# One layer of a hybrid attention and state-space network: decay rows read from HBM and merged by a masked copy, a rotary turn by halves, a later division, silu(z) kept in HBM

## The chip, the cores and the metric

The kernel runs on one core of a Trainium2 chip. The metric is the device time of one execution in microseconds; the figure given is the median of three runs. The core has a matmul engine (TensorE, PE in the profile, with its weight loads as PEld), a vector engine (VectorE, DVE), an activation engine (ScalarE, ACT), a general engine (GpSimd, POOL), a queue that mostly issues DMAs (SyncE, SP) and 16 DMA engines. SBUF is its working memory, PSUM the memory that matmuls write, HBM the large memory outside.

## The reference

One layer on 512 latent tokens of width 1024, with a prefix of 256 context tokens; all in float32, depth 1. Cut to what matters:

```
h = modulate(rms_norm(x), shift, scale) @ w_in      # cq, ckv, kr, z, xbc, dt; the same for the context
# 16 attention heads: 64 columns without and 32 with rotary position, 512 queries on 768 keys
q_rope = q_rope * cos + rotate_half_axial(q_rope) * sin
p = softmax((q_nope @ k_nope.T + q_rope @ k_rope.T) * SCALE);  attn = p @ v
# 16 state-space heads, forward and backward, chunks of 128 tokens
cum = cumsum(dt * A)                                # within a chunk
y = (C B^T * tril(exp(cum_t - cum_s))) @ (dt * xs)  # y_diag: decay inside a chunk, per head and direction
  + exp(cum_t) * (C @ entering_state)               # y_off
y = y_forward + flip(y_backward) + d * xs
ssd = rms_norm(y * silu(z))
x = x + gate * rms_norm(concat(attn, ssd) @ w_out)
x = x + gate * rms_norm((gelu(conv(g)) * v) @ w_down)   # gated MLP, g and v from one product with w_up
```

The forward decay of a head is nonzero for s <= t, the backward one for s >= t; both hold the diagonal s = t.

## The kernel before, in words

Almost every product is made in three passes of float32r matmuls: a helper `split` (L495 to L498) cuts an operand into a high part (ScalarE copies it) and a low part (VectorE subtracts), and high x high, high x low and low x high are added up in PSUM. So each operand costs ScalarE and VectorE one pass over it. Transposes and a few small products run on unsplit float32.

The program is written as generators. It is traced twice: the first trace collects all instructions, then `plan` (L381) schedules them by its own price list, orders each engine's instructions and gives every tile a place in SBUF. Memory is counted in units of 256 float32 columns; `t2` takes two units and `t4` four, UNITS is their number. The written order decides which tile may follow which in a place; the order of the instructions on each engine is the plan's.

The stages in order: modulation and the z part of the input projection (`silu_of_z`, L687, keeps the values of silu(z), doubled, in four `t4` tiles `z` until the scan ends); the other parts of the projection; then two generators beside each other (`beside`, L453): `group_sums`, the scan of both groups of eight state-space heads with `ssd_finish`, and `projections`, the rest of the input projection and then eight pairs of attention heads. `beside(main, other, pace)` steps the second by the weight that the first yields, times `pace`. After both comes the output projection (`natural_gemm`, attention's rows first), the gated MLP's up products and its down products.

The places that the change touches:

- The decay of head h on two chunks (L1019 to L1040). Two matmuls with `sel` spread the rows of the running sums `chl` (a high and a low part) over 128 partitions, for the two directions (L1025). A third one (L1029, identity x `caps`) adds -1e30 where a direction has no decay. ScalarE takes the exponential of four 128x128 blocks with a bias by column (L1034), GpSimd adds the two directions (L1038), VectorE multiplies with C B^T (L1039). The result `M` is the operand of y_diag (L1058).
- The states (L997 to L1018) are computed first; the entering states of all chunks and directions are kept, and their products (L1048 to L1054) are made after the decays, beside y_diag. `y` is `z` itself, multiplied in place (L1062).
- The rotary turn of the queries (L1119 to L1126): a float32 matmul with a matrix `rot` of zeros, ones and minus ones per two head pairs (L1122), then products with cosine and sine and their sum.
- The attention of a head (L1167 to L1182): scores in PSUM, their largest value (VectorE, L1177), the exponential and its sum (ScalarE, L1179), the reciprocal (L1181) and the division of the 128x768 weights by it (GpSimd, L1182), then six transposes (L1193), a split, and the product with V (L1205).
- The rows of the modulation (`modfinish`, L1267): a column tile of 8 values on 128 partitions goes to HBM in single words and comes back as a row on all partitions, both issued by GpSimd.

## Time and profile before

| what | value |
|---|---|
| three runs | 999.69, 1001.02, 1004.33 us |
| median | 1001.02 us |
| span of the profiled execution (first to last instruction) | 994.4 us |
| mean granted clock of TensorE | 0.990 |
| DVE, ACT, POOL busy | 700.9, 501.4, 259.5 us |
| DMA | 116.88 MB, 118 GB/s in the mean |

The page gives the span of the profiled execution and no device time of its own, so the span stands beside the runs. In the groups of instructions a row reads: line, engine, operation, tile written<-tiles read, their shapes, count | busy us, mean ns of one | idle us of the engine before them, and what ended it. An engine's busy time counts overlapping instructions once; matmuls follow each other more closely than their duration says. A line such as L498 is a helper's and stands for all its callers; the shapes tell these apart.

### The profile page before, as it was taken

The numbers are of one execution on the slowest core, as the hardware profiler recorded it, in microseconds if no ns is written. First come the engines' busy times: TensorE is split into PE (matmuls) and PEld (weight loads), VectorE is DVE, ScalarE is ACT, GpSimd is POOL, SyncE is SP. The second block draws the span as 40 slices with busy tenths as digits, with TensorE's granted clock in tenths as the row PEclk, the third lists the DMA queues.
The fourth block names the chain that finished last, engine by engine and source line by source line (L and its number), as shares of the span: only waits on it lengthen the run. The fifth ranks groups of instructions, "written<-read, shape, count | busy, mean of one in ns | idle before, by whom it ended". The sixth has DMA issues, their size and how long they took to land.

```text
span 994.4 us, 14412 instructions
## 1 busy us (share of the span) xinstructions
PE 971.8 (98%) x5224; PEld 825.9 (83%) x5224; DVE 700.9 (70%) x1304; ACT 501.4 (50%) x994; POOL 259.5 (26%) x223
## 2 busy tenths in 40 slices
PE   9999999999998999999999999999999999999996
PEld 8888888888876888888888888888888888888885
DVE  5999866988896989978789997952515442773406
ACT  4545337568566787687787324842314323452101
POOL 0001001765697886656541000000000000000000
PEclk7999999999998999999999999999999999999999
DMA  9922101012222242331566965431223221354422
GB/s 350 362 74 85 53 1 44 22 48 81 67 57 54 56 111 78 99 74 46 153 259 230 323 160 199 148 127 64 106 85 106 106 85 43 110 177 137 158 76 84
DMA packets 42214, 116.88 MB, mean 118 GB/s; under 512 B 5776, under 2 KB 8736, under 8 KB 42144
## 3 DMA queue, kind: packets, MB, share of 16 engines
q1 hardware_dynamic: 41440, 114.30, 34.8%
q0 software_dynamic: 528, 1.59, 0.5%
q8 instruction: 41, 0.67, 0.3%
q14 instruction: 29, 0.24, 0.1%
q10 hardware_dynamic: 176, 0.09, 0.0%
HBM read 96.02 MB, written 4.21 MB: 101 GB/s over the span
## 4 chain that ended last, share of the span: by engine, by line
PE 49%; DVE 6%; DMA 4%; issue 2%; ACT 1%; SPq 0%; POOL 0%; DVEq 0%; ACTq 0%; POOLq 0%
PE banks L751 26%; PE banks L1476 12%; PE banks L1175 4%; PE banks L1205 3%; PE banks L1193 2%; DVE block L498 2%; DMA block<-block 1%; DMA mod_rows<-mod 1%; DVE block L586 1%; PE banks L1109 1%; DMA block<-mod_rows 1%; ACT block L1179 1%; DVE smalls L1177 1%; DMA block<-in_wmod_dram 0%; DVE smalls L524 0%
## 5 line engine op out<-in xcount | busy, mean ns | idle before, releaser
L751 PE MATMUL banks<-block,block 128*128 128x512 f32 (+1 forms) x2132 | 448.3, 360 | 1.7 <-DVE block L1385 1.1
L751 PEld LDWEIGHTS banks<-block,block 128*128 128x128 f32 x2132 | 358.8, 188 | 62.5 <-issue 1.6
L498 DVE TENSOR_TENSOR block<-block,block 128x512 fp32r<-128x512 f32 (+5 forms) x252 | 227.0, 923 | 125.7 <-PE banks L751 47.8
L497 ACT ACTIVATE block<-block 128x512 fp32r<-128x512 f32 (+5 forms) x252 | 181.4, 743 | 207.8 <-PE banks L751 48.1
L1476 PE MATMUL banks<-block,block 128*128 128x512 f32 x496 | 116.6, 389 | 0.0
L1182 POOL TENSOR_TENSOR block<-block,smalls 128x768 f32<-128x768 f32 x64 | 97.3, 1527 | 60.7 <-DVE smalls L1181 38.4
L1476 PEld LDWEIGHTS banks<-block,block 128*128 128x128 f32 x496 | 93.0, 188 | 19.5
L1175 PE MATMUL banks<-block,block 128*128 128x512 f32 (+1 forms) x384 | 95.1, 357 | 1.4 <-DMA block<-block 0.7
L1276 POOL DMA_DIRECT2D mod_rows<-mod x3 | 2.9, 975 | 351.4 <-DVE mod L1272 351.4
L498 DVE TENSOR_TENSOR block<-banks,block 128x256 fp32r<-128x256 f32 (+1 forms) x156 | 83.2, 555 | 14.7 <-ACT block L497 12.9
L497 ACT ACTIVATE block<-banks 128x256 fp32r<-128x256 f32 (+1 forms) x156 | 73.0, 498 | 32.4 <-PE banks L1193 17.7
L1289 PE MATMUL banks<-block,block 128*128 128x512 f32 x384 | 88.6, 390 | 0.0
L1289 PEld LDWEIGHTS banks<-block,block 128*128 128x128 f32 x384 | 71.8, 188 | 14.5
L1193 PE MATMUL banks<-cst,block 128*128 128x128 f32 x384 | 66.9, 279 | 4.1 <-DVE block L498 3.7
L1205 PE MATMUL banks<-block,block 128*128 128x256 f32 x384 | 68.7, 299 | 0.8 <-DVE block L498 0.8
L1175 PEld LDWEIGHTS banks<-block,block 128*128 128x128 f32 x384 | 59.6, 190 | 10.2 <-ACT block L1179 2.7
L586 DVE SCALAR_TENSOR_TENSOR block<-block,block 128x1024 f32<-128x1024 f32 x52 | 62.6, 1219 | 4.1 <-DMA block<-in_wmod_dram 1.9
L1177 DVE TENSOR_REDUCE smalls<-banks 128x1 f32<-128x768 f32 x64 | 60.8, 950 | 6.6 <-PE banks L1175 5.9
L1179 ACT ACTIVATE block<-banks,smalls 128x768 f32<-128x768 f32 x64 | 57.7, 902 | 13.2 <-DVE smalls L1177 7.6
L786 DVE SCALAR_TENSOR_TENSOR block<-banks,cwh,block 128x510 f32<-128x510 f32 (+3 forms) x88 | 51.1, 620 | 14.4 <-ACT block L782 13.9
L1205 PEld LDWEIGHTS banks<-block,block 128*128 128x128 f32 x384 | 55.9, 191 | 5.3 <-DVE block L498 1.1
L1193 PEld LDWEIGHTS banks<-cst,block 128*128 128x128 f32 x384 | 47.7, 143 | 14.1 <-DVE block L498 3.9
(216 smaller groups left out, 1064.1 us busy)
## 6 DMA issues: line engine op xcount, KB each, us to landing
block<-in_wmod_dram SPq DMA_DIRECT2D x48, 512.0 KB, 6.9
block<-in_wup_dram SPq DMA_DIRECT2D x44, 512.0 KB, 3.8
block<-in_wdn_dram SPq DMA_DIRECT2D x44, 256.0 KB, 2.8
block<-block SPq DMA_DIRECT2D x32, 256.0 KB, 3.0
block<-in_wout_dram SPq DMA_DIRECT2D x16, 512.0 KB, 5.9
block<-block SPq DMA_DIRECT2D x56, 128.0 KB, 2.3
block<-in_wxbc_dram SPq DMA_DIRECT2D x12, 512.0 KB, 3.4
block<-in_wz_dram SPq DMA_DIRECT2D x16, 256.0 KB, 7.1
```

The costliest lines, as they stand in the source:

```text
L497: act(hi, src, AF.Copy)
L498: (lo_eng or V).tensor_tensor(out=lo, in0=src, in1=hi, op=ALU.subtract)
L586: V.scalar_tensor_tensor(out=junk, in0=wt, scalar=0.5, in1=vec, op0=ALU.mult, op1=ALU.mult, accum_out=acc)
L751: mm(po, lhsT=wf(k, pt[0]), rhs=xf(k, pt[1]), start=(k == 0 and pt == parts[0]), stop=(k == nk - 1 and pt == parts[-1]))
L1175: mm(sc[:, o : o + n], lhsT=q_[:, x_, qi * P : (qi + 1) * P], rhs=kk[:, y_, :], start=part == 0, stop=part == 2)
L1177: V.reduce_max(nm, sc[:, :T], axis=AX.X, negate=True)
L1179: act(pe, sc[:, :T], AF.Exp, bias=nm, scale=1.0, accum_out=sm_)
L1182: G.tensor_tensor(out=pe, in0=pe, in1=sm_.to_broadcast([P, T]), op=ALU.mult)
L1193: nc.tensor.transpose((tx if c < NX else tc_)[:, o : o + P], pe[:, s_ : s_ + P], ident)
L1205: mm(po[:, half * 256 : half * 256 + 256], lhsT=vst(c), rhs=rhs, start=(part == 0 and c == 0), stop=(part == 1 and c == NKT - 1))
L1289: mm(po[i][:, nh * 512 : nh * 512 + 512], lhsT=l[lp][:, i * P : (i + 1) * P], rhs=w[wp][:, nh * 512 : nh * 512 + 512], start=(k == 0 and l ...
L1476: mm(po[i], lhsT=l[lp][:, i * P : (i + 1) * P], rhs=w[wp], start=(k == 0 and lp == 0 and wp == 0), stop=(k == NF - 1 and lp == 1))
```

## The change

Five edits and what belongs to them:

- Decays. The running sums of both directions are copied to HBM as 32 rows (`cum_rows`). For each head and pair of chunks a DMA brings the head's two rows, spread over all partitions, as a tile of 128 x 2 x 256. VectorE adds to the forward part, for each chunk, a column (`nbd`, the difference of the two directions' biases), then a masked copy puts the forward part over the backward one where s <= t. ScalarE takes the exponential of the two merged blocks with the backward bias, GpSimd multiplies with C B^T. The backward term of the diagonal, which the merged decay no longer holds, goes into the factor of xs: dt_backward x diag(C B^T) + d (`skip`).
- The products with the entering states are made as soon as a state is known, and added up in `yc`; the states are not kept.
- Rotary. The 32 rotary columns of queries and keys are reordered in the weights so that the partner of a row lies 64 partitions away; two VectorE products of half height read one half of PSUM and write the other. Each head's rotary rows are then copied in two pieces.
- Division. The exponentials go undivided into the product with V. The eight sums of a pair of heads are inverted at once, stored to HBM in single words, read back as rows and multiplied into the 128x512 result by GpSimd.
- silu(z) is stored to HBM when it is made and read back, 128x512 at a time, where `y` is formed.

The rows of the modulation are issued by ScalarE's queue. UNITS goes from 200 to 212 and the scratch of dynamic DMAs to 4096 bytes; the pace of `beside` goes from 1.0 to 1.5. The mask matrices `capf` and `capb` go. The diff, cut to its core:

```diff
-UNITS, EDGE, MARGIN = 200, 168, 2500
+UNITS, EDGE, MARGIN = 212, 168, 2500
+PACE, MW = 1.5, 1.5
...
-        zi = z[i][:, nh * 512 : nh * 512 + 512]
+        zi = t2()
         act(zi, po[i], AF.Tanh, scale=0.5)
         V.scalar_tensor_tensor(out=zi, in0=zi, scalar=1.0, in1=po[i], op0=ALU.add, op1=ALU.mult)
+        load(gate[nh, i], zi)
...
-    act(chl[:32], pq[:32], AF.Copy)
-    V.tensor_tensor(out=chl[32:64], in0=pq[:32], in1=chl[:32], op=ALU.subtract)
+    act(cumT, pq[:32], AF.Copy)
+    load(cumR.rearrange("d h t -> (d h) t"), cumT)
...
                 if n >= 2:
-                    entering[dir_][c] = state[dir_]
+                    ep = t2(P, 512, dt=F32R), t2(P, 512, dt=F32R)
+                    split(*ep, state[dir_], V)
+                    pO = pget("s")
+                    for part, (i, j_) in enumerate(((0, 0), (1, 0), (0, 1))):
+                        mm(pO, lhsT=cp_[:, i, c * P : (c + 1) * P], rhs=ep[j_], start=part == 0, stop=part == 2)
...
-                pdf = pget("s")
-                for dir_ in range(2):
-                    mm(pdf[:, dir_ * 256 : dir_ * 256 + 256],
-                       lhsT=sel[:, dir_ * 16 + h : dir_ * 16 + h + 1].to_broadcast([P, P]),
-                       rhs=chl[:, cp2 * 256 : cp2 * 256 + 256], start=dir_ == 0, stop=False)
-                mm(pdf, lhsT=capi, rhs=caps, start=False, stop=True)
-                df = t2()
-                for dir_ in range(2):
-                    for j in range(2):
-                        o = (dir_ * 2 + j) * P
-                        act(df[:, o : o + P], pdf[:, o : o + P], AF.Exp,
-                            bias=nb[:, cp2 * 2 + j, dir_ * 16 + h : dir_ * 16 + h + 1])
-                G.tensor_tensor(out=Me, in0=df[:, :256], in1=df[:, 256:], op=ALU.add)
-                V.tensor_tensor(out=Me, in0=Me, in1=cbt[:, cp2 * 256 : cp2 * 256 + 256], op=ALU.mult)
+                df, at = t2(P, 2, 256), slice(cp2 * 256, cp2 * 256 + 256)
+                load(df, cumR[:, h, at].unsqueeze(0).to_broadcast([P, 2, 256]))
+                for j in range(2):
+                    V.tensor_scalar(out=cols(0, j), in0=cols(0, j), scalar1=nbd[:, cp2 * 2 + j, h : h + 1], scalar2=None, op0=ALU.add)
+                V.copy_predicated(df[:, 1, :].rearrange("p (c n) -> p c n", c=2), later, df[:, 0, :].rearrange("p (c n) -> p c n", c=2))
+                for j in range(2):
+                    act(cols(1, j), cols(1, j), AF.Exp, bias=nb[:, cp2 * 2 + j, 16 + h : 17 + h])
+                G.tensor_tensor(out=M[e // 4][:, e % 4, :], in0=df[:, 1, :], in1=cbt[:, at], op=ALU.mult)
...
-                G.tensor_tensor(out=y[c][:, gs], in0=y[c][:, gs], in1=ya, op=ALU.mult)
+                zl = t2()
+                load(zl, gate[g, c])
+                G.tensor_tensor(out=y[c][:, gs], in0=zl, in1=ya, op=ALU.mult)
...
+            for to, of in ((slice(0, 64), slice(64, 128)), (slice(64, 128), slice(0, 64))):
+                V.tensor_tensor(out=qsn[to], in0=pq[of], in1=C("sin")[to], op=ALU.mult)
             pfree(pq)
-            pr = pget("p")
-            mm(pr, lhsT=C("rot"), rhs=qr, start=True, stop=True)
-            V.tensor_tensor(out=qsn, in0=pr, in1=C("sin"), op=ALU.mult)
...
-            r0 = ((hp % 2) * 2 + j) * 32
-            nc.sync.dma_start(out=r32(qt[j][64:96]), in_=r32(qrs[r0 : r0 + 32]))
+            r0 = ((hp % 2) * 2 + j) * 16
+            for o in range(2):
+                nc.sync.dma_start(out=r32(qt[j][64 + 16 * o : 80 + 16 * o]), in_=r32(qrs[64 * o + r0 : 64 * o + r0 + 16]))
...
-        act(pe, sc[:, :T], AF.Exp, bias=nm, scale=1.0, accum_out=sm_)
+        act(pe, sc[:, :T], AF.Exp, bias=nm, scale=1.0, accum_out=sum_)
-        V.reciprocal(out=sm_, in_=sm_)
-        G.tensor_tensor(out=pe, in0=pe, in1=sm_.to_broadcast([P, T]), op=ALU.mult)
...
+        V.reciprocal(out=sums, in_=sums)
+            nc.sync.dma_start(out=back.rearrange("n p -> p n"), in_=sums)
+        nc.sync.dma_start(out=inv, in_=back.rearrange("(j n) p -> j (n p)", j=2).unsqueeze(1).to_broadcast([2, 64, S]))
+        G.tensor_tensor(out=at, in0=at, in1=inv, op=ALU.mult)
...
-    beside(group_sums(), second, 1.0)
+    beside(group_sums(), second, PACE)
...
-            G.dma_start(out=scratch[n].rearrange("j p -> p j"), in_=ms)
+            nc.scalar.dma_start(out=scratch[n].rearrange("j p -> p j"), in_=ms)
-        G.dma_start(out=row, in_=scratch[n : n + 1].rearrange("o j p -> o (j p)").to_broadcast([P, D]))
+        nc.scalar.dma_start(out=row, in_=scratch[n : n + 1].rearrange("o j p -> o (j p)").to_broadcast([P, D]))
```

More of the change, by code (lines that the diff above doesn't have):

```diff
@@ L679, in build @@
     pfree(pw)
-    z = [t4() for _ in range(NX)]
+    gate = nc.dram_tensor("gate_rows", (2, NX, P, 512), F32, kind="Internal").ap()
     def half_of_z(nh, po, wz, k, i):
@@ L1041, in ssd @@
+                yield MW
             for j in range(2):
                 c = cp2 * 2 + j
[L1043 to L1054 removed]
@@ L1055, in ssd @@
-                yield 3
+                ya = yc[c]
                 yd = pget("s")
@@ L1214, in pair_of_heads @@
         at = attn[hp // 2][:, hp % 2, :]
+        sums, inv = small("sums", 2 * NX), t2()
+        back = nc.dram_tensor(f"sums_{hp}", (2 * NX, P), F32, kind="Internal").ap()
         for j in range(2):
@@ L1221, in pair_of_heads @@
                 for q2 in range(2):
-                    transposed(*scores(heads[j], half * 2 + q2), pT, q2)
+                    transposed(*scores(heads[j], half * 2 + q2, sums[:, j * NX + half * 2 + q2 :][:, :1]), pT, q2)
                     yield 1.9
@@ L1518, in lay_out @@
     wq = g["w_q_up"][0].reshape(384, NH, 96)
+    turn = np.array([i % 8 + 16 * (i % 16 // 8) + 8 * (i // 16) for i in range(32)])
+    wqr = wq[:, :, 64 + turn].reshape(384, 4, 4, 2, 16).transpose(0, 1, 3, 2, 4).reshape(384, 512)
     wkv = g["w_kv_up"][0].reshape(256, NH, 128)
```

95 lines of the change are left out of this document (47 added, 48 removed).

## The prediction

> **What bounds the kernel now.** I read the page first, then the busy time by stretches, the chain of waits for the spacing of back-to-back matmuls, and the groups of instructions of the stretch that the change edits.
>
> ```profile
> span 994.4 us, 14412 instructions
> ...
> PE 971.8 (98%) x5224; PEld 825.9 (83%) x5224; DVE 700.9 (70%) x1304; ACT 501.4 (50%) x994; POOL 259.5 (26%) x223
> ```
>
> TensorE is busy for 98% of the span. The three runs have a median of 1001.02 us; the page gives the span alone for the execution that it profiled, so I carry 6.6 us (1001.0 less 994.4) for what lies around it and add it back at the end.
>
> Nearly all that is edited runs between 190 and 528 us: the scan of the state-space heads and the attention beside and after it. The columns below are stretch, length, then busy time of PE, PEld, DVE, ACT and POOL, the granted clock, the share of the DMA engines and GB/s.
>
> ```profile
> core 0: us, PE busy (x) PEld busy (x) DVE busy (x) ACT busy (x) POOL busy (x), PEclk, DMA share, GB/s
> 190.00:528.00 338.00, 326.86 (x2034) 280.79 (x2032) 289.27 (x528) 253.39 (x590) 227.00 (x183) 0.99 0.32 90
> 260.00:320.00 60.00, 53.89 (x299) 43.97 (x298) 48.90 (x76) 39.66 (x94) 53.73 (x44) 0.94 0.27 68
> 632.00:852.00 220.00, 220.00 (x1077) 186.18 (x1077) 97.43 (x122) 75.45 (x103) 0.00 (x0) 1.00 0.26 90
> ```
>
> Here no engine is free: VectorE is busy for 86% of the 338 us, ScalarE for 75%, GpSimd for 67%. In the worst part, 260 to 320 us, GpSimd is the one that is full (53.73 of 60) and the clock falls to 0.94. From 632 us on TensorE alone counts; nothing is edited there that could shorten it.
>
> A busy matmul is not one at its peak, so I take the spacing of matmuls that follow each other in the chain of waits (start, length, what, count):
>
> ```profile
> 399.67 0.86 PE banks L1122 x2
> ...
> 406.53 0.65 PE banks L1193 x6
> 407.19 0.84 PE banks L1058 x8
> ...
> 450.81 1.43 PE banks L1205 x12
> ...
> 569.81 11.20 DMA mod_rows<-mod
> ...
> 877.88 108.21 PE banks L1476 x477
> ```
>
> So a 512-column matmul takes 108.21/477 = 0.227 us, a 256-column one 1.43/12 = 0.119, a transpose 0.108, a product of L1058 0.105, and a record of the rotary matmul L1122 0.43. The matmuls of the stretch from 190 to 528 us, with their counts:
>
> ```profile
> L751 PE MATMUL banks<-block,block 128*128 128x512 f32 x260 | 79.5, 402 | 0.6 <-ACT block L497 0.6
> L1205 PE MATMUL banks<-block,block 128*128 128x256 f32 x360 | 64.8, 299 | 0.8 <-DVE block L498 0.8
> L1193 PE MATMUL banks<-cst,block 128*128 128x128 f32 x370 | 64.6, 279 | 4.1 <-DVE block L498 3.7
> L1175 PE MATMUL banks<-block,block 128*128 128x512 f32 x192 | 63.4, 414 | 0.3 <-DMA block<-block 0.3
> L1175 PE MATMUL banks<-block,block 128*128 128x256 f32 x192 | 37.5, 299 | 1.1 <-DMA block<-block 0.4 <-ACT block L1179 0.4
> L751 PE MATMUL banks<-block,block 128*128 128x256 f32 x172 | 29.6, 285 | 0.0
> L1109 PE MATMUL banks<-block,block 128*128 128x512 f32 x72 | 21.3, 403 | 0.0
> L1058 PE MATMUL banks<-block,block 128*128 128x64 f32 x128 | 17.2, 267 | 0.4 <-DVE block L1052 0.3
> L1050 PE MATMUL banks<-block,block 128*128 128x512 f32 x48 | 15.6, 403 | 0.0
> L1025 PE MATMUL banks<-block,sel 128*128 128x256 f32 x64 | 14.6, 301 | 0.4 <-ACT block L1034 0.4
> L1029 PE MATMUL banks<-block,capi 128*128 128x512 f32 x32 | 12.9, 402 | 0.0
> L1010 PE MATMUL banks<-block,block 128*128 128x512 f32 x37 | 12.6, 429 | 3.3 <-DVE block L1015 2.5 <-ACT block L1162 0.6 <-ACT block L1012 0.2
> L1082 PE MATMUL banks<-cst,block 128*128 128x128 f32 x32 | 5.4, 276 | 0.0
> L801 PE MATMUL banks<-cst,block 128*128 128x128 f32 x30 | 4.7, 272 | 0.0
> L1122 PE MATMUL banks<-block,cst 128*128 128x512 f32 x8 | 4.1, 592 | 0.0
> ```
>
> There are 641 of 512 columns (145.5 us), 788 of 256 (93.8), 432 transposes (46.7), 128 of L1058 (13.4) and 8 of L1122 (3.4): 303 us of work in 338. The shortfall is 35 us: 11 us that the stretch shows as idle (338 less 326.86), the rest inside matmuls that stand waiting. That is the room for this change, beside the matmuls that it deletes.
>
> **What leaves TensorE.** The two spreading matmuls and the mask matmul of each decay go: 64 x 0.119 + 32 x 0.227 = 7.6 + 7.3 us. The four rotary matmuls go: 8 x 0.43 = 3.4. Nothing is added to TensorE; the products with the entering states move to an earlier place but keep their number. Sum: 18.3 us, all on the path wherever TensorE is the bound. Its work in the stretch becomes 303 - 18 = 285 us.
>
> **ScalarE and GpSimd.**
>
> ```profile
> L1034 ACT ACTIVATE block<-banks,block 128x128 f32<-128x128 f32 x128 | 40.0, 373 | 8.7 <-PE banks L1029 8.3 <-POOL block L1038 0.2
> ```
> ```profile
> L1182 POOL TENSOR_TENSOR block<-block,smalls 128x768 f32<-128x768 f32 x64 | 97.3, 1527 | 60.7 <-DVE smalls L1181 38.4 <-PE banks L1193 9.8 <-PE banks L1205 3.8
> L1038 POOL TENSOR_TENSOR block<-block 128x256 f32<-128x256 f32 x32 | 28.4, 889 | 26.2 <-ACT block L1034 20.5 <-DVE block L797 4.8 <-PE banks L1175 0.9
> ```
>
> Only the merged decay is raised to a power, so 64 of the 128 exponentials go: 24 us of ScalarE. GpSimd loses the 64 divisions of the weights (97.3 us) and gets one 128x512 product for each of eight head pairs instead, about 8 x 1.0 = 8 us at the rate of L1182 (1527 ns for 768 columns); its addition L1038 becomes a product of the same size. GpSimd falls from 227 to some 140 us of 338 and stops being the full engine at 260 to 320 us. The division also sat in the row of steps from the scores to the transposes: 0.16 us of reciprocal and 1.5 us of product less per block of 128 queries.
>
> **VectorE.** This is where the change pays.
>
> ```profile
> L498 DVE TENSOR_TENSOR block<-block,block 128x512 fp32r<-128x512 f32 x41 | 40.9, 1000 | 4.9 <-issue 1.5 <-ACT block L1162 1.3 <-ACT block L497 0.8
> ...
> L1039 DVE TENSOR_TENSOR block<-block,block 128x256 f32<-128x256 f32 x32 | 19.5, 629 | 0.6 <-POOL block L1038 0.6
> ...
> L1230 DVE TENSOR_TENSOR block<-banks,block 64x512 f32<-64x512 f32 x14 | 9.6, 686 | 1.9 <-ACT block L1229 1.5
> L1181 DVE RECIPROCAL smalls<-smalls 128x1 f32<-128x1 f32 x63 | 9.4, 156 | 10.1 <-ACT block L1179 9.7
> ```
>
> It loses L1039 (19.5) and L1181 (9.4). It gains 64 additions of a column to a 128x128 block. No row shows one; they lie between a reciprocal of one column (0.16) and half of L1039 (0.31), and I take 0.20, near the lower: 12.8 us. It gains 32 masked copies of 128x256, which no row shows either: at least L1039's mean of 0.629 less what it loses to GpSimd, say 0.41, at most two such passes, 1.26; I take 0.63, since it too streams two operands from SBUF: 20.1 us (13 to 40). The rotary turn in halves makes eight half-height products of four full ones: 4 x 0.69 = 2.8. The diagonal's correction, the column difference and the reciprocals by eight columns come to about 4 us at 0.15 to 0.7 each. Against that, 41 subtractions of two SBUF operands take 1.000 us where the same 512 columns with one operand in PSUM take 0.69 (L1230): 13 us lost while GpSimd works. GpSimd loses 87 of 227 us, so I give back 5. Sum: 289.3 - 28.9 + 12.8 + 20.1 + 2.8 + 4 - 5 = 295 us (285 to 322 with the ends of both unknown prices).
>
> The Trainium skill, VectorE: DVE Perf Modes, The perf-mode tier table, says that a float32 operation with one SBUF operand and a scalar runs at two elements a cycle; worked out with that page's 58 cycles of fixed cost, 128 columns are an estimate of 0.13 us. By that the 64 additions are 8 us and the engine's sum 290 instead of 295; no row of this trace shows one of that size.
>
> So after the change VectorE (295) and TensorE (285) are equally the bound. How two full engines go together shows in two stretches of the output projection (columns as before):
>
> ```profile
> 564.00:573.00 9.00, 9.00 (x41) 7.47 (x40) 9.00 (x15) 1.70 (x2) 1.08 (x1) 1.00 0.92 315
> 574.00:583.00 9.00, 9.00 (x42) 7.45 (x40) 9.00 (x18) 0.68 (x1) 0.57 (x1) 1.00 0.35 57
> ```
>
> Both are full at once there, with a clock of 1.00; but in the edited stretch the steps depend on each other. I take VectorE 94 to 95% busy: a stretch of 312 us instead of 338, **26 us less**. Of these, 18 are the deleted matmuls and 8 come out of the shortfall (35 to 27).
>
> **DMA and queues.**
>
> ```profile
> L1153 SPq DMA_DIRECT2D block<-block x16: 507/545/597, 268.7 to 490.6; - x16
> ```
> ```profile
> block<-block SPq DMA_DIRECT2D x32, 256.0 KB, 3.0
> ...
> held_rows<-block SPq DMA_DIRECT2D x4, 512.0 KB, 2.9
> ...
> mod_rows<-mod POOLq DMA_DIRECT2D x3, 4.0 KB, 10.3
> ```
>
> SP issues 81 more: 32 loads of decay rows, one store of them, 8 stores and 8 loads of silu(z), 16 more half copies of the rotary rows, 16 for the sums. At 0.545 us that is 44 us on a queue that has 338 and more; behind each stand weight loads, which are issued ahead. The row loads bring 32 x 256 KB = 8.4 MB, and z comes back with 2.1, on a stretch that moves 90 GB/s x 338 us = 30 MB, while 315 GB/s are reached between 564 and 573 us. A row load should land some 3.0 us after its issue, as a copy of 256 KB does, and needs no engine, and the freed 16 units of z, the 12 new ones and the mask tiles give it room ahead of its use. I cost them at nothing; without that room each of 32 would show up to 3 us.
>
> The rows of the modulation move from GpSimd's queue to ScalarE's. ScalarE then waits in order for the column's landing (10.3 us); behind it stand the splits of the output weights. In the two stretches quoted it is busy for 2.4 us of 18, so this is covered: 0, with up to 10 us if it is not, or 2 less if the hardware queue starts sooner. Storing z falls where TensorE works without pause: 0. The interleaving at pace 1.5 shifts scan work later into attention; its effect is inside the 27 us of shortfall that remain.
>
> Sum: 994.4 - 26 = 968.4 of span, **975 us** as a time.
>
> **Rivals.** *VectorE sets the pace.* For it: 295 us of work is more than it has now, and the additions and masked copies could cost 20 us more. Against it: the stretch at 564 us, where it is full and TensorE too. At 0.90 busy the stretch is 328 us and the time 991; at today's 0.856 it is 345, and 1008. Chance 0.22; of that 0.12 faster, 0.07 same, 0.03 slower.
>
> *The shortfall nearly goes.* For it: GpSimd was the full engine in the worst 60 us, where the clock fell too. Then 15 us stay: a stretch of 300, and 963 us. Against it: VectorE at 98%. Chance 0.12.
>
> *The word stores dry the DMA queues* (the slower side). Each pair stores 1024 sums as single words, as the modulation columns do now. One such store is issued by the chain at 569.81 us, and between the two stretches quoted above the traffic falls from 315 to 57 GB/s, for some 7 us. Eight stores make 56 us in which copies between heads, row loads and weights behind them stand still. If TensorE sits through more than half of that, the 26 us are gone; at three quarters (42) the time is 1017. Against it: TensorE was full in these 9 us, and the quotients of a pair are not wanted before the output projection, so the stores can go when the queue is slack. Chance 0.08, of which 0.07 slower. The Trainium skill, DMA: Bandwidth & Descriptors, Specifications, puts the limit for line rate at runs of 512 bytes and says that shorter ones make the engine read, modify and write. By that rule the trace agrees: 4 KB in words land after 10.3 us, 512 KB in rows after 2.9.
>
> **How the numbers follow.** The forecast has 0.58, with 966 to 984 as its own range (VectorE between 286 and 305 us). Its 975 stands as the time. The range 958 to 996 takes in the second rival and most of the first, and leaves out the third and the tail of the first, some 0.17. A measurement of this kernel can tell 0.5% from no change, so faster is under 996: 0.58 + 0.12 + 0.12 = 0.82. Same: 0.07 and 0.01 of the third, 0.08. Slower: 0.03 + 0.07 = 0.10.
>
> **What would show it.** Right: the stretch from the scan's start to the output projection's is near 312 us; GpSimd near 140 us there; no part has a clock under 0.99; VectorE is over 90% busy, masked copies near 0.63 us and additions near 0.20. Wrong: masked copies over 1 us with TensorE waiting on VectorE; matmuls waiting on row loads or copies just after a store of sums; ScalarE waiting at the row of the modulation with TensorE idle after 570 us; or a stretch from 632 us on that is longer, which I hold to be untouched.

## The result, and the profile after

| | median | runs | ratio to before |
|---|---|---|---|
| before | 1000.36 us | 999.63 to 1004.33 | |
| after | 1041.9 us | 1037.8 to 1046.76 | 1.0399 [1.036, 1.0437] |

The change makes the kernel 4% slower. The forecast said 975. The page of after: its span, the busy engines, the granted clock in 40 slices and the DMA packets.

```profile
span 1044.9 us, 14163 instructions
...
PE 979.8 (94%) x5120; PEld 829.8 (79%) x5120; DVE 702.3 (67%) x1326; ACT 483.5 (46%) x928; POOL 161.7 (15%) x157
...
PEclk6999999999899999989999999899999999999999
...
DMA packets 65909, 131.52 MB, mean 126 GB/s; under 512 B 18176, under 2 KB 29456, under 8 KB 65840
```

Three terms close the sum. The matmul work, counted with the spacings of the prediction, fell by 18.3 us as forecast. TensorE's idle time (span less busy) rose from 994.4 - 971.8 = 22.6 to 65.1 us, by 42.5. The clock lost 1.0% of 994.4 us before, 9.9 us, and 3.8% of 1044.9 now, 39.7, or 29.8 more. Together that is +54 against a measured +50.5 in span; the two last terms overlap, since in some of the idle time the clock is low too (worked out from the two traces, the overlap grew by 3.7 us). So TensorE has less to do and stands still more often, and after the gaps it runs slower for a while. The spans exaggerate the loss: the profiled execution of after is the slowest of its four runs, that of before was a quick one (994.4 and the 1.9 us that time and span of after are apart make an estimated 996.3, under all its runs), and the medians lie 41.5 us apart.

Busy time of after by stretches, columns as before:

```profile
core 0: us, PE busy (x) PEld busy (x) DVE busy (x) ACT busy (x) POOL busy (x), PEclk, DMA share, GB/s
190.00:560.00 370.00, 330.16 (x1977) 282.66 (x1976) 301.59 (x566) 242.83 (x537) 145.65 (x137) 0.95 0.48 115
230.00:276.00 46.00, 35.48 (x179) 28.64 (x177) 38.41 (x76) 22.55 (x51) 19.14 (x17) 0.96 0.59 154
400.00:530.00 130.00, 114.02 (x708) 98.48 (x708) 97.97 (x212) 90.89 (x208) 37.50 (x40) 0.95 0.59 125
566.00:620.00 54.00, 48.17 (x201) 38.97 (x200) 43.33 (x68) 12.64 (x15) 4.30 (x3) 0.94 0.77 223
655.00:676.00 21.00, 14.07 (x90) 13.26 (x90) 18.96 (x68) 14.19 (x38) 1.27 (x1) 0.76 0.36 126
700.00:900.00 200.00, 200.00 (x919) 166.74 (x919) 91.28 (x116) 62.68 (x79) 0.00 (x0) 1.00 0.30 107
```

The edited stretch is 370 us long and not 312, and in it no engine is full: TensorE 89%, VectorE 82%, ScalarE 66%, GpSimd 39%. That looks like waiting for something that is not an engine. The groups of after that the prediction priced:

```profile
L1175 PE MATMUL banks<-block,block 128*128 128x512 f32 (+1 forms) x384 | 99.8, 372 | 21.0 <-DMA block<-block 7.8 <-DMA block<-cum_rows 5.8 <-ACT block L1179 4.1
...
L1048 POOL TENSOR_TENSOR block<-block,block 128x256 f32<-128x256 f32 x31 | 24.6, 801 | 58.9 <-ACT block L1047 49.2 <-DVE block L1044 8.9 <-PE banks L1203 0.4
...
L1047 ACT ACTIVATE block<-block,block 128x128 f32<-128x128 f32 x64 | 22.0, 401 | 5.2 <-DVE block L1045 3.7 <-issue 1.5
...
L1044 DVE TENSOR_SCALAR block<-block,block 128x128 f32<-128x128 f32 x60 | 17.1, 321 | 8.5 <-DMA block<-cum_rows 8.5
...
L1045 DVE COPY_PREDICATED block<-block,block 128x256 f32<-128x256 int32 x32 | 14.3, 462 | 0.0
...
L1236 POOL TENSOR_TENSOR block<-block,block 128x512 f32<-128x512 f32 x8 | 11.4, 1429 | 81.1 <-DMA block<-sums 58.8 <-DVE block L583 22.2
```

L1175, the scores, had 0.7 us of idle time for DMAs before (0.3 and 0.4 in its two rows) and has 13.6 now. That is all of TensorE's idle time that ends, by the profile, with a DMA; most of the rest ends with VectorE or ScalarE, and whether a late DMA stands behind those gaps has to be followed up or settled by runs. The DMA issues of after say which transfers are late (median us from issue to landing at the end of a row):

```profile
block<-in_wmod_dram SPq DMA_DIRECT2D x48, 512.0 KB, 10.4
...
block<-cum_rows SPq DMA_DIRECT2D x32, 256.0 KB, 6.2
block<-block SPq DMA_DIRECT2D x32, 256.0 KB, 4.4
block<-in_wout_dram SPq DMA_DIRECT2D x16, 512.0 KB, 10.3
...
block<-sums SPq DMA_DIRECT2D x8, 256.0 KB
```

A decay row takes 6.2 us and not 3.0; the copies between heads went from 3.0 to 4.4; the weights of the output projection from 5.9 (before) to 10.3. And while one of the eight rows of sums is loaded, this is the whole traffic of the core (after, columns as above):

```profile
573.00:577.00 4.00, 3.64 (x9) 2.87 (x10) 3.83 (x7) 1.38 (x3) 0.00 (x0) 0.50 0.12 47
```

A DMA share of 0.12 is 2 of 16 engines, and 47 GB/s is theirs. The load writes two blocks of 64 partitions, and its outermost dimension has the size 2. The Trainium skill, DMA: Bandwidth & Descriptors, Rules for kernel authors, states that the slowest dimension of a pattern sets how many engines carry a DMA. The row agrees. At 47 GB/s 256 KB take an estimated 5.6 us, and in that row next to nothing else moves. The granted clock there is 0.50.

One gap can be followed through. From 565 to 568 us another of these loads is nearly all that moves. ScalarE waits 6.54 us for weights of the output projection; behind their split stands its step L1229, behind that VectorE's L1230, and TensorE waits 4.36 us for it (after, columns as above; then lines of the three engines' timelines: start, length, what, and in brackets the wait before it):

```profile
565.00:568.00 3.00, 3.00 (x18) 2.59 (x17) 2.59 (x5) 0.00 (x0) 0.00 (x0) 1.00 0.13 51
```
```profile
570.90 1.06 ACT L494 ACTIVATE block<-block 128x1024 fp32r<-128x1024 f32 x1 [6.54 <-DMA block<-in_wout_dram]
571.99 0.59 ACT L1229 ACTIVATE block<-banks 64x512 f32<-64x512 f32 x1
572.61 0.69 DVE L1230 TENSOR_TENSOR block<-banks,block 64x512 f32<-64x512 f32 x1 [5.02 <-ACT block L1229]
573.36 11.85 PE L1294 MATMUL banks<-block,block 128*128 128x512 f32 x39 [4.36 <-DVE block L1230]
```

A decay row stands in the way in another manner. SP's queue of after, then TensorE, in the largest single gap:

```profile
435.29 0.53 SPq L486 DMA_DIRECT2D block<-cum_rows  x1
435.87 1.17 SPq L1149 DMA_DIRECT2D block<-block  x1
437.13 0.53 SPq L486 DMA_DIRECT2D block<-cum_rows  x1
438.31 0.51 SPq L1155 DMA_DIRECT2D block<-block  x1
438.87 0.58 SPq L486 DMA_DIRECT2D block<-cum_rows  x1
441.30 0.48 SPq L1156 DMA_DIRECT2D block<-block  x1
```
```profile
436.83 1.09 PE L749 MATMUL banks<-block,block 128*128 128x512 f32 x4
443.75 1.65 PE L1175 MATMUL banks<-block,block 128*128 128x512 f32 x3 [5.83 <-DMA block<-cum_rows]
```

The rows alternate on one queue with the copies that an attention head needs before its scores (L1149 to L1156), so by the profile the head waits for rows that are not its own. Rows issued by another queue were not tried, so that their place on this queue is the harm is argued, not shown.

### The profile page after: what moved, and what is told of

Same layout as the page of the kernel before. It is cut to its first block, busy times and chain, and to the rows that moved or that the text cites. A ratio compares the mean times of both kernels' runs of the same rounds, so it can differ in the third digit from the quotient of the medians.

```text
span 1044.9 us, 14163 instructions
## 1 busy us (share of the span) xinstructions
PE 979.8 (94%) x5120; PEld 829.8 (79%) x5120; DVE 702.3 (67%) x1326; ACT 483.5 (46%) x928; POOL 161.7 (15%) x157
## 5 line engine op out<-in xcount | busy, mean ns | idle before, releaser
L749 PE MATMUL banks<-block,block 128*128 128x512 f32 (+1 forms) x2132 | 456.0, 366 | 12.8 <-ACT block L1389 4.1
L749 PEld LDWEIGHTS banks<-block,block 128*128 128x128 f32 x2132 | 365.1, 192 | 78.8 <-issue 6.0
L494 ACT ACTIVATE block<-block 128x512 fp32r<-128x512 f32 (+4 forms) x252 | 181.3, 743 | 260.0 <-PE banks L1481 40.6
L495 DVE TENSOR_TENSOR block<-block,block 128x512 fp32r<-128x512 f32 (+4 forms) x252 | 216.7, 883 | 101.1 <-ACT block L494 45.1
L1481 PE MATMUL banks<-block,block 128*128 128x512 f32 x504 | 119.2, 394 | 3.0 <-DVE block L1426 3.0
L1175 PE MATMUL banks<-block,block 128*128 128x512 f32 (+1 forms) x384 | 99.8, 372 | 21.0 <-DMA block<-block 7.8
L1481 PEld LDWEIGHTS banks<-block,block 128*128 128x128 f32 x504 | 96.0, 191 | 23.5 <-DVE block L1426 3.4
L1294 PE MATMUL banks<-block,block 128*128 128x512 f32 x384 | 92.5, 399 | 5.8 <-DVE block L1230 4.4
L495 DVE TENSOR_TENSOR block<-banks,block 128x512 fp32r<-128x512 f32 (+1 forms) x156 | 83.7, 556 | 15.1 <-ACT block L494 14.6
L1294 PEld LDWEIGHTS banks<-block,block 128*128 128x128 f32 x384 | 73.5, 193 | 21.8 <-DVE block L1230 4.8
L1175 PEld LDWEIGHTS banks<-block,block 128*128 128x128 f32 x384 | 62.5, 200 | 31.1 <-DMA block<-block 10.8
L1203 PE MATMUL banks<-block,block 128*128 128x256 f32 x384 | 71.3, 298 | 1.7 <-DVE block L1230 1.3
L1179 ACT ACTIVATE block<-banks,smalls 128x768 f32<-128x768 f32 x64 | 57.6, 900 | 26.0 <-DVE smalls L1177 21.6
L1203 PEld LDWEIGHTS banks<-block,block 128*128 128x128 f32 x384 | 58.4, 194 | 7.0 <-issue 2.2
L779 DVE SCALAR_TENSOR_TENSOR block<-banks,cwh,block 128x510 f32<-128x510 f32 (+3 forms) x88 | 52.4, 622 | 11.9 <-ACT block L775 11.1
L1426 DVE TENSOR_TENSOR block<-banks,block 128x512 f32<-128x512 f32 x22 | 14.9, 687 | 65.8 <-PE banks L749 65.8
L1191 PEld LDWEIGHTS banks<-cst,block 128*128 128x128 f32 x384 | 47.3, 143 | 11.9 <-DVE block L495 6.1
L681 PE MATMUL banks<-block,block 128*128 128x512 f32 x192 | 54.2, 410 | 0.0
## 6 DMA issues: line engine op xcount, KB each, us to landing
block<-in_wout_dram SPq DMA_DIRECT2D x16, 512.0 KB, 10.3
```

The costliest lines, as they stand in the source:

```text
L494: act(hi, src, AF.Copy)
L495: (lo_eng or V).tensor_tensor(out=lo, in0=src, in1=hi, op=ALU.subtract)
L681: mm(po[i], lhsT=hx[k][:, hp, i * P : (i + 1) * P], rhs=wz[wp], start=(k == 0 and wp == 0 and hp == 0), stop=(k == KD - 1 and hp == 1))
L749: mm(po, lhsT=wf(k, pt[0]), rhs=xf(k, pt[1]), start=(k == 0 and pt == parts[0]), stop=(k == nk - 1 and pt == parts[-1]))
L1175: mm(sc[:, o : o + n], lhsT=q_[:, x_, qi * P : (qi + 1) * P], rhs=kk[:, y_, :], start=part == 0, stop=part == 2)
L1179: act(pe, sc[:, :T], AF.Exp, bias=nm, scale=1.0, accum_out=sum_)
```

## The experiments

Nothing of the computation is left out in any of them. Each is a separate program that is planned anew, so all instructions may move; e18 shows how much that alone can do. The theory before the runs: late DMAs, on the one hand the load of the sums, on the other the decay rows. Rivals: the stores in single words, VectorE's added work, the plan's pace, the new queue of the modulation's rows.

**e1, the division as before the change.**

```diff
-        V.reciprocal(out=sums, in_=sums)
...
-        nc.sync.dma_start(out=inv, in_=back.rearrange("(j n) p -> j (n p)", j=2).unsqueeze(1).to_broadcast([2, 64, S]))
-        G.tensor_tensor(out=at, in0=at, in1=inv, op=ALU.mult)
...
+        V.reciprocal(out=sm_, in_=sm_)
+        G.tensor_tensor(out=pe, in0=pe, in1=sm_.to_broadcast([P, T]), op=ALU.mult)
```

> The changed kernel with the division of the weights before the product with V put back (reciprocal and GpSimd product per 128 queries), and so without the stores of sums as words and the loads of their rows; all other edits stay. Theory W (the words and their row loads dry the DMA queues, TensorE stands and its clock falls): the droughts after 340 us are gone, time 1041.9 falls by 25 to 40 us, to 1002 to 1017. Theory D (the 32 loads of decay rows hold up the copies between heads): the falls of the clock before 450 us stay, time within 10 us of 1041.9. Theory P (the pace of 1.5 and the new plan are at fault): within 10 us too.

Measured: 1022.81 us, ratio 1.0256 [1.0214, 1.0298]. The late division loses 19 us, although it takes 87 us off GpSimd; that lies between the expectations. More than half of the loss is elsewhere.

**e2, the decays as before** (two spreading matmuls, mask matmul, 128 exponentials; no rows through HBM).

> The changed kernel with the decays spread by matmuls with sel and the mask matmul again, so without the rows through HBM, the masked copy and the diagonal's correction; all other edits stay. It has 14.9 us more of TensorE work. Theory D: the gaps at 272, 385 and 437 us go, time falls by 15 to 25 us in spite of the added work, to 1017 to 1027. Theory W: the time rises by some 10 to 15 us, since the added matmuls come on top, or stays within 5. Theory P: the same as W.

Measured: 1041.27, 1.044 [1.0391, 1.0489]: no gain in time. This does not clear the decays: e2 has 14.9 us of matrix work more, so about as much waiting went with the rows (worked out as in the table below, TensorE is 20 us less behind its work at 980 us than in after). In the waits of TensorE in e2 (total, times, longest) one of 7.5 us ends, by the profile, with a load of sums:

```profile
PE banks L1178 <- DMA block<-sums: 7.5, 1, 7.5
```

**e3, the pace.** `PACE` from 1.5 to 1.0.

> The changed kernel with the pace at 1.0 as before; nothing else. Theory P: time falls by 20 us or more. Theories W and D: within 10 us of 1041.9, since the stores, loads and their number stay.

Measured: 1029.69, 1.032 [1.0278, 1.0361], 12 us less: between the two expectations.

**e4, the sums' load in two halves**, words stored as they are:

```diff
-        nc.sync.dma_start(out=inv, in_=back.rearrange("(j n) p -> j (n p)", j=2).unsqueeze(1).to_broadcast([2, 64, S]))
+        rows_ = back.rearrange("(j n) p -> j (n p)", j=2)
+        for j in range(2):
+            nc.sync.dma_start(out=inv[64 * j : 64 * j + 64], in_=rows_[j : j + 1].to_broadcast([64, S]))
```

> The changed kernel with the row load of the inverted sums made as two loads of 64 partitions each in place of one whose outer dimension is 2; the word stores stay. If the load runs on two of the 16 DMA engines now (50 KB a microsecond at 564 to 568 us), each of the eight falls from about 5 us to under 2. Theory W with half of its weight on these loads: time falls by 8 to 15 us. If the word stores alone matter: within 5 us. Theories D and P: within 5 us.

Measured: 1022.53, 1.025 [1.0195, 1.0304]: 19 us less, more than expected and as much as undoing the whole division. The outermost dimension is now 64.

**e8, no words either:** TensorE turns the 128x8 sums, eight rows of 512 bytes are stored, and the load is that of e4.

```diff
+        nc.tensor.transpose(turned[: 2 * NX, :P], sums, ident)
+        act(rt, turned[: 2 * NX, :P], AF.Copy)
...
+        nc.sync.dma_start(out=back, in_=rt)
```

> The changed kernel with the sums turned to rows by one transpose on TensorE for each pair (8 x 0.1 us) and stored as eight rows of 512 bytes, and the row load made as two loads of 64 partitions: no word stores of sums and no two-engine loads. Theory W (words): 5 to 15 us faster than the run with the two loads alone (1022.5), so 1008 to 1018. If the two-engine load was all of the sums' cost: 1019 to 1026.

Measured: 1021.38, 1.0208 [1.0171, 1.0245], the same as e4. The landing of the halves in e4, then in e8:

```profile
block<-sums SPq DMA_DIRECT2D x16, 128.0 KB, 8.3
```
```profile
block<-sums SPq DMA_DIRECT2D x16, 128.0 KB, 3.0
```

Without words the rows come 5 us sooner, and it is worth 1 us, within the spread of the runs. So the price of the late division was the load by two engines and not the stores in words. The two halves that e8 issues at 561.4 and 561.9 us pass in 1.8 us, with 0.88 of the engines busy, other traffic included (e8, columns as above):

```profile
562.90:564.70 1.80, 1.80 (x10) 1.49 (x9) 1.80 (x3) 1.80 (x3) 0.00 (x0) 1.00 0.88 222
```

**e5 and e6, division and decays as before,** at pace 1.5 and at 1.0.

> The changed kernel with both the division and the decays as before; what stays is the rotary turn by halves, silu(z) in HBM, the early products with the entering states, 212 units, the pace of 1.5 and the modulation rows on ScalarE's queue. If the two transfers through HBM (sums and decay rows) are the whole loss, it has TensorE's work less only 3.4 us and the time is 990 to 1002. If each hides the other's loss, so that removing one alone gave 19 and 1 us, the same. If the pace or the order is a cause of its own, it stays over 1010.

> The kernel of the run before this, with the pace at 1.0. If the pace costs by itself (12 us with everything else changed), this is 8 to 14 us faster than the run with the pace of 1.5. If the pace only cost because it put the transfers of the scan and of the attention beside each other for longer, the two are within 4 us of each other.

Measured: 1004.52, 1.0043 [1.0018, 1.0069], and 997.13, 0.9981 [0.9953, 1.001]. What is left of the change in e6 (rotary halves, silu(z) in HBM, early products with the states, units, modulation rows) costs nothing that can be measured. From e1 to e5 the time falls by 18 us although 14.9 us of matrix work come back, so some 33 us of waiting go with the decay rows; from after to e2 it was some 15. What the rows cost depends on what else is waited for. The pace costs 7 us here, a little less than expected.

**e7, the modulation's rows back on GpSimd's queue.**

> The changed kernel with the modulation rows issued by GpSimd as before; nothing else. If ScalarE's wait for the column (11.5 us at L1346, then 10 us at half the clock after 661 us) costs on the path, the time falls by 8 to 15 us from 1041.9. If the column lands as late from either queue and the stretch is late for another reason, within 4 us.

**e16, the same beside a late division that works** (e10 below).

> As e10_late_division_turned (993.8 us), the rows of the modulation on GpSimd's queue again. If GpSimd's queue itself is the slower one: 1000 to 1005 us, as in e7_rows_gpsimd, where it cost 10 us. If it was slower there only because the stores of sums stood in the way: 992 to 996 us.

Measured: e7 1052.56, 1.0523 [1.0495, 1.0551], 11 us slower than after and outside both expectations; e16 1000.83, 1.0022 [0.9988, 1.0056], 7 us slower than e10. The move to ScalarE was no fault. That GpSimd's queue is the slower one isn't shown either: e16 issues the first of these rows at 573 us, and TensorE is by 566 us already 12 us further behind its work than in e10 (worked out as in the table below) and regains 5 of them later. So it may be the other plan.

**e10, decays as before, late division with turned sums, pace 1.0.**

> Decays as before the change, division of the product with V as in the changed kernel, its sums turned by TensorE and stored as 8 rows of 512 bytes and loaded in halves of 64 partitions, pace 1.0. Against e6_both_back_pace_one (997.13 us) only the division differs. Theory L (the load that two engines carry was the whole price of the late division): 985 to 998 us, since GpSimd has 97 us less to do. Rival W (any round trip of the sums through HBM holds the product with V back): over 1004 us, with matmuls waiting behind the load of the sums.

Measured: 993.8, 0.9915 [0.9883, 0.9948]. Once its sums come by all engines the late division no longer loses. That it gains is not shown: 3 us less than e6 is within what a new plan alone can do (e18). It has the lowest median of the kernels without needless work, with e15 and e17 some 2 us behind.

**e13 and e11, the decay rows in the plan.** Both are e8 at pace 1.0; e11 also tells the planner that a load of decay rows takes 2500 ns.

```diff
+        if ops[-1][0] == "cum_rows":
+            return 2500
         return DMA_WORDS if words else size(ops[0]) * ops[0][1][0][1] * 4 / 360
```

> The changed kernel with the sums turned (e8_sums_turned, 1021.38 us) and pace 1.0; e11_rows_priced_in_plan (1002.04 us) is the same with a price of 2500 ns on the decay rows. Theory P (the price moved the users away from their loads): 1007 to 1012 us, the pace alone giving about 12 us as in e3_pace_one and the price the rest. Rival: the pace gave it all, 1000 to 1004 us.

> The changed kernel with the sums turned by TensorE (as e8_sums_turned, 1021.38 us), pace 1.0, and each load of decay rows priced at 2500 ns in the plan, so that the plan lets their users fall later. Theory P (the plan puts the users of the rows too close behind their loads): 995 to 1006 us. Rival H (the loads take queue and engines from the weights, wherever the plan puts them): 1008 to 1018 us, the pace alone giving some 10 us.

Measured: e13 1013.14, 1.0136 [1.0079, 1.0193]; e11 1002.04, 1.0009 [0.9976, 1.0043]. e13 lies just above both of its expectations. The pace gives 8 us, the third gain of 7 to 12, and the price 11 more. The planner had 256 KB / 360 = 0.73 us for the transfer; with its own allowances (`DMA_START`, `DMA_WAIT`, `DMA_ALONE`) it counted on 2.9 us from the end of the issue to the first use, and with 2500 ns it counts on 6.1. The rows of e13 land 5.7 us after their issue. So the old price put the users too near; that this is what the 11 us are rests on one pair of plans.

**e9, the spread by matmuls kept, merged by a masked copy; no row through HBM** (e6 otherwise, 7 us less matrix work).

```diff
-                load(df, cumR[:, h, at].unsqueeze(0).to_broadcast([P, 2, 256]))
+                for dir_ in range(2):
+                    mm(pdf[:, dir_ * 256 : dir_ * 256 + 256],
+                       lhsT=sel[:, dir_ * 16 + h : dir_ * 16 + h + 1].to_broadcast([P, P]),
+                       rhs=chl[:, at], start=True, stop=True)
+                act(df[:, 1, :], pdf[:, 256:], AF.Copy)
                 for j in range(2):
-                    V.tensor_scalar(out=cols(0, j), in0=cols(0, j), scalar1=nbd[:, cp2 * 2 + j, h : h + 1], scalar2=None, op0=ALU.add)
+                    V.tensor_scalar(out=cols(0, j), in0=pdf[:, j * P : (j + 1) * P], scalar1=nbd[:, cp2 * 2 + j, h : h + 1], scalar2=None, op0=ALU.add)
```

> Against e6_both_back_pace_one (997.13 us) this kernel changes only the decays: the matrix work that spreads the running sums stays in two products, the mask product is dropped, and the masked copy merges the spread rows in PSUM; no row goes through HBM. The division stays as before the change. TensorE has about 7 us less work than in e6. Theory H (the wait for the decay rows, which land 5.2 to 6.2 us after issue, is what the decays lose): with the load gone the merge costs nothing, 985 to 997 us. Rival M (the merge itself, masked copy on VectorE and subtraction on GpSimd ahead of the exponential, is late for the matmuls): 1000 to 1015 us, with matmuls waiting on the exponentials or on VectorE's copies.

Measured: 1009.93, 1.0097 [1.0064, 1.013], 13 us slower than e6 (the subtraction on GpSimd that the expectation speaks of is the product with C B^T, which stays there). Busy time by stretches of e9, columns as before: from 300 to 400 us VectorE is the fullest engine, at 94.5%. But e6 has it at 91.4% there, with TensorE at 96.0%, so this alone doesn't show that VectorE is the cause.

```profile
300.00:400.00 100.00, 88.90 (x521) 73.13 (x520) 94.53 (x188) 70.80 (x174) 78.12 (x68) 0.98 0.34 85
```

**e12, this merge with the late division of e10; e14, the same with the column added by ScalarE** while it moves the forward rows out of PSUM; **e15, e11 with the additions on ScalarE.**

```diff
-                    V.tensor_scalar(out=cols(0, j), in0=cols(0, j), scalar1=nbd[:, cp2 * 2 + j, h : h + 1], scalar2=None, op0=ALU.add)
+                    act(cols(0, j), cols(0, j), AF.Identity, bias=nbd[:, cp2 * 2 + j, h : h + 1])
```

> The merge of e9_spread_merge_no_hbm and the turned late division of e10_late_division_turned together, pace 1.0: no decay row through HBM, the sums through HBM in rows of 512 bytes. If both theories H and L hold, this is the fastest kernel, 975 to 992 us, below the kernel before. If M or W holds it is above 1003 us.

> As e12_merge_and_late_division (1001.19 us), but VectorE no longer adds the column: ScalarE moves the forward rows from PSUM with the column as bias, in two pieces of 128 columns, in place of its copy of the backward rows, and VectorE merges with one masked copy that takes the backward rows out of PSUM (the diagonal then holds the backward decay, and the factor of xs the forward one). VectorE loses 64 additions, some 20 us of its 305 in 190 to 530 us. Theory V (VectorE's steps of the merge hold TensorE back): 984 to 994 us, at or below e10_late_division_turned (993.8), with 7 us less matrix work than it. Rival C (the length of the chain from spread to product, whichever engine carries it): 998 to 1004 us.

> As e11_rows_priced_in_plan (1002.04 us), the 64 additions of the column moved from VectorE to ScalarE. Theory V: VectorE loses some 19 of its 308 us in 190 to 530 us, 990 to 997 us. Rival H (the landing of the rows is what is left): 999 to 1004 us.

Measured: e12 1001.19, 0.9996 [0.9962, 1.0029], between its two expectations; e14 1000.66, 1.0008 [0.9976, 1.0039]; e15 996.25, 0.9969 [0.9932, 1.0005]. In e14 20 us less of VectorE give nothing, in e15 they give 6. VectorE's additions are not what holds the merge back in PSUM; for the rows in HBM it stays unclear, since 6 us is less than what e18 shows for a mere replanning.

**e17, the price at 4500 ns, and e18, each row loaded twice,** the second time into a tile that nobody reads; both otherwise e15.

> As e15_rows_priced_adds_on_scalar (996.25 us), the price of a load of decay rows in the plan 4500 ns instead of 2500, near what these loads take (5.7 us from issue to landing, which the plan's own allowances come on top of). Theory P (late rows are part of what is left): 986 to 994 us. Rival Q (the rows come in time already, and what is left are the copies between heads that come late beside them): 994 to 1001 us.

> As e15_rows_priced_adds_on_scalar (996.25 us), every load of decay rows made twice, the second into a tile that nobody reads: 8.4 MB and 32 issues more. Theory H (the bytes and packets of the rows hold up the copies between heads and the weights): 1004 to 1020 us. Rival: the transfers themselves cost nothing while the plan knows them, 993 to 1001 us.

Measured: e17 995.56, 0.9966 [0.9933, 0.9999]; e18 989.5, 0.9898 [0.9864, 0.9933]. More price gives nothing. Twice the traffic makes the kernel 7 us *faster*, against both expectations, and the fastest of all. Busy time by stretches of e18: from 400 to 530 us it carries 202 GB/s, and TensorE is nearly full, where after had 125 GB/s and 114.02 us busy.

```profile
400.00:530.00 130.00, 127.79 (x874) 113.58 (x874) 109.18 (x186) 107.45 (x232) 19.25 (x20) 1.00 0.73 202
```

So the bytes and packets of the decay rows, even doubled, need not hold TensorE back. That leaves their place in the order, which e11 against e13 points to. And a needless load cannot itself save 7 us, so the plan that it happened to bring did: steps of this size between two plans (e12, e14, e15, e17 among each other, e16, e10 against e6) say nothing of their edits.

How far TensorE has fallen behind its own work, worked out from each trace (time less the work done by then, with the spacings of the prediction), in us:

| by | 190 | 276 | 400 | 530 | 620 | 700 | 980 |
|---|---|---|---|---|---|---|---|
| before | 12.4 | 16.0 | 35.0 | 43.6 | 43.6 | 47.0 | 46.8 |
| after | 17.1 | 35.5 | 57.6 | 86.3 | 98.6 | 109.4 | 115.5 |
| e8, sums turned | 14.1 | 34.8 | 56.7 | 81.7 | 82.5 | 90.1 | 90.1 |
| e13, and pace 1.0 | 15.2 | 34.0 | 68.2 | 75.8 | 78.0 | 80.5 | 80.6 |
| e11, and rows priced | 13.7 | 32.3 | 48.6 | 56.1 | 60.6 | 69.2 | 70.4 |
| e10, decays by matmul | 11.9 | 17.2 | 29.6 | 37.3 | 42.7 | 46.8 | 46.4 |

The loss from 530 us on belongs to the sums' load, which falls into the output projection's weights: after loses 29 us there and e8 8. (The median landing of these weights doesn't tell it: 9.4 us in e4 and 5.6 in e8, which take the same time.) At pace 1.5 the other runs with the undivided load lose 22 (e2) and 35 us (e7), e4 with the halves 11. Between 276 and 530 us the price of the rows acts: 42 us in e13, 24 in e11. The loss up to 276 us looks like that of the decays in these rows, but isn't shown to be: e1 and e7 keep the decay rows and are 24 and 25 us behind by then, and e5, without them, 27.

## Why the prediction was wrong

**The step that failed** is "I cost them at nothing", said of the 81 added issues and their loads, and with it the 8 us that were to come out of the shortfall "(35 to 27)". Two reasons stood behind it. The one, that a row load lands after 3.0 us "as a copy of 256 KB does", took the bytes as the measure: the decay rows landed after 6.2, and the sums' load, of the same bytes, ran on two engines at 47 GB/s. The other, room ahead through freed units, counted memory; the order of issue is the plan's, and the plan counted on the rows 2.9 us after their issue. Runs e4 and e8 put the sums' load at 19 to 21 us; e3, e6 and e13 put the pace, which I took to lie inside the shortfall, at 7 to 12; e13 and e11 put the place of the rows at 11, on one pair of plans. With these three, from after to e11, the time falls from 1041.9 to 1002.04 us, though each step is also a new plan.

**Matrix work,** 18.3 us less: right by count. The time did not follow, because 69 us more of gaps and slow clock came on top (46.8 to 115.5 us behind in the table).

**GpSimd,** 227 to some 140: 145.65, right. Its product of a head pair took 1.429 us and not 1.0. **ScalarE,** 24 us less: 40.0 became 22.0, so 18; the 64 exponentials took 0.401 us each.

**VectorE,** 295 us: 301.59 in a longer stretch, right as a sum by errors against each other. The additions took 0.321 us, not 0.20 (up to 0.502, in e1); the masked copies 0.462, not 0.63 (0.44 to 0.65 in other runs). The subtractions of two SBUF operands fell from 1.000 to 0.831 us with GpSimd less busy, some 7 us for the 41 of them, where 5 were given back. The estimate of 0.13 us for an addition that the prediction took from the Trainium skill, VectorE: DVE Perf Modes, was further off; here the trace decides.

**"VectorE 94 to 95% busy"** was the wrong way to get a length of stretch: it was 82%, and TensorE 89%: neither was what the other waited for throughout. The test by two stretches of the output projection did not hold for a stretch whose steps hang on DMAs.

**The modulation's rows,** "up to 10 if it is not" covered: ScalarE did wait 11.5 us for the landing, and the stretch 655 to 676 us has TensorE busy for 14.07 of 21 with a clock of 0.76. But e7 and e16 are no better with GpSimd's queue, and e6 and e10 lose little there with ScalarE's, so the queue isn't the cause. What makes that stretch late stays open; the sign listed for it, ScalarE waiting at the row with TensorE idle after 570 us, did come true.

**From 632 us on,** untouched: right in its middle (700 to 900 us is full at 1.00), wrong at its start, where the stretch 655 to 676 us loses 7 us of TensorE's time and some clock, and a little after 900 us: from 700 to 980 us TensorE falls 6 us further behind.

**The rivals.** *VectorE sets the pace:* not in the changed kernel, where it is 82% busy. With the rows out of HBM it is fuller (e9), but taking 20 us off it there gave nothing (e14). *The word stores* came nearest: right that the sums dry the queue while output weights are wanted. Of the sign listed for it half came true: matmuls wait on row loads and copies, but not just after a store of sums (before the gap at 438 us the last one is at 399). And its part was the wrong one: e4 keeps the words, e8 drops them, both take the same time, and the load behind the store was the fault. At 0.08 I gave it too little, for the reason that quotients are not wanted early; the harm is to others' transfers, not to the quotients. That the pace and the price of a new load in the planner could matter was in no rival.

**The 6.6 us** carried for what lies around the span were too many: in the profiled execution of after, time and span are 1046.76 and 1044.9 us, 1.9 apart. The rest of the 6.6 would be a quick profiled execution. Set against a miss of 67 us this is small.

## What to carry to other kernels

Price a DMA by its shape, not by its bytes: the size of its outermost dimension decides between 2 engines at 47 GB/s and all of them, and splitting each of eight such loads into two halves of 64 partitions gave back 19 us. Work moved to DMA isn't free because engines have time: ask which transfers share its queue, who stands behind them, and what the scheduler believes the load takes. And where a planner reorders everything, measure how far two plans of the same computation lie apart (7 us here, from one pair) before reading a cause into a smaller step.

## What was not expected of the hardware

- A gap is paid again by the clock: 42.5 us more idle time came with 29.8 us more lost to it. The row at 573 us shows the granted clock at 0.50. The Trainium skill, TensorE: Matmul & The Clock Gate, Part 1, gives half rate after an idle window of about 3.4 us. The slow periods of after last 3.4 to 17.1 us, the longest at the start of the program; but a stretch with 2.45 us of idle time in all was enough for one (after, columns as above):

```profile
517.00:521.00 4.00, 1.55 (x12) 1.27 (x12) 0.68 (x1) 3.00 (x6) 0.00 (x0) 1.00 0.39 39
521.00:524.50 3.50, 3.50 (x16) 3.21 (x15) 2.69 (x5) 2.76 (x5) 0.00 (x0) 0.52 0.23 18
```

- A masked copy of 128x256 from SBUF took 0.462 us in after (0.44 to 0.65 in other runs), against 0.629 for a product of the same shape in the kernel before.
- Two rows of 1 KB spread over 128 partitions took 4.7 us to land in e11 and 5.7 in e13 and e15, against 3.0 to 3.2 us for a copy of the same 256 KB between tiles in these kernels.
- A store of 1024 words took 9.9 us to land in e4, and yet doing without it (e8) gained nothing that can be measured once the load behind it was well shaped.
